# Front of a two-layer decoder trunk on one Trainium2 core: memory norms from rows, low parts on VectorE, keys in side banks, an earlier x

## The chip, the cores and the metric

The kernel runs on one core of a Trainium2 chip. The core has TensorE (PE, matrix multiply, with weight loads listed as PEld), VectorE (DVE), ScalarE (ACT), GpSimd (POOL) and SyncE (SP, which here issues loads), an on-chip memory SBUF of 128 partitions, and eight accumulator banks (PSUM) of 128 x 512 floats that PE writes and VectorE and ScalarE read. Each engine works through its own queue in order and waits on semaphores for the others. The metric is the device time of one execution in microseconds, as a median of several.

## What is computed

Two layers of a hybrid decoder trunk over a sequence of 256 tokens of width 1024, with 256 memory tokens. Per layer:

```python
h = rms_norm(x, norm_g[l])
proj = h @ w_in[l]                                  # 1024 x 5120: ten groups of 512 columns
q_a, k_a, v_a, q_h, f_h, i_h, q_m, z = jnp.split(proj, split_points, axis=-1)
...                                                 # o_a: causal attention; o_h: gated linear recurrence
kv_m = rms_norm(mem, mem_norm_g[l]) @ w_mem_kv[l]   # 1024 x 1024
k_m, v_m = jnp.split(kv_m, 2, axis=-1)
km = rms_norm(k_m.reshape(B, M, MEM_HEADS, MEM_HEAD_DIM), mem_k_norm[l])
vm = v_m.reshape(B, M, MEM_HEADS, MEM_HEAD_DIM)
...                                                 # o_m: attention of qm over km, vm
y = jnp.concatenate([o_a, o_h, o_m], axis=-1) * jax.nn.silu(z)
x = x + y @ w_out[l]
```

`rms_norm` divides each row by the root of its mean square. For the memory this factor (`rm` in the kernel) is one number per memory token. The kernel multiplies un-normalised memory with the weights and applies `rm` afterwards, to the values directly and to the keys inside their own norm.

## The kernel before

**Precision and tiles.** All products are made in three passes from a high part (rounded to the type `fp32r`) and a low part (the difference, rounded likewise). Every weight tile is 128 x 1024 floats (512 KB) and passes through three steps in a fixed order of tiles: a load by SyncE into one of four `wr` buffers (`dma_to`, L124), a cast on ScalarE into one of three `wh` buffers (`h_to`, L141, instructions at L147 and L150), and the low part on VectorE into one of three `wl` buffers (`l_to`, L153, instructions at L159 and L162). `slot` (L190) asks for loads five tiles, casts three tiles and low parts two tiles ahead of the tile in use. A load into a `wr` buffer waits until the low part of the tile four before is made.

**Order of the work.** The first eight tiles are the memory's key and value weights of layer 0 (`group_kv`): the memory, transposed on the host (`mem_t`) and split into `mTh` and `mTl` (`m_split`, L351 and L352), is the stationary operand; key columns go to two accumulator banks, value columns to two more. There are four main banks (`acc`) and four side banks (`sd`). In layer 0 keys and values both take main banks, so all four are taken; in layer 1 the keys take side banks. Then `group_a` makes the projection's forget gate and query of the recurrence, each in four column tiles of 128 columns, one main bank each; `g_sum` empties a bank. Eight more groups, the output projection, and the second layer follow.

**Side work.** Everything that is not a large product is a Python generator (`spawn`), advanced one step at each `slot`. It only sets the order in which the program is written; a planner then orders the instructions of each engine by its own estimate of their durations. Instructions marked with `keep_in_program_order` keep their order among themselves: all loads, the spread of the norm, and some others.

**The front's side work**, in the order that matters here:

- `g_norm0` (L399 to L435) makes `h` of layer 0. Squares of `x`'s rows with sums on ScalarE (L403), a scale on VectorE (`msx`, L411), a power on GpSimd (`rx`, L412), a diagonal on VectorE (`dg`, L417), one product with a matrix of ones on PE that spreads the row factors along the columns of a side bank (L420). Then for each of eight 128-column blocks VectorE multiplies the transposed `x` (`xc`, loaded from `x_t`) by gain and factor (L427), ScalarE makes the high part (L431) and GpSimd the low part (L432) of `hT`, the operand of every projection.
- `g_mem_r` (L371 to L397) makes `rm`. Squares of the transposed memory on ScalarE (L376), sums over blocks on GpSimd (L379, L381), four one-column products with ones on PE that sum over partitions, a scale on VectorE (L389), a power on GpSimd (L391). `rm2` (L393, L394) goes to the keys' norm.
- `g_km` (from L602) copies the keys out of their banks (L605 on VectorE, L606 on ScalarE), takes their norm, and transposes them on PE (L636). `g_vm` (from L644) waits for `rm` and empties the value banks (L650 on ScalarE, L651 on VectorE).

**Loads.** SyncE issues in program order: the memory and the first weight tiles interleaved, up to six weight tiles, then `x` in two halves, the first half of `x_t`, the seventh and eighth weight tile, the second half of `x_t`, and from there weight tiles as their buffers come free.

Of the kernel before, what the change touches and what calls it, by code (L numbers as in the profile page):

```python
# [12 lines left out]
F32 = mybir.dt.float32  # L13
# [9 lines left out]
D = 1024  # L23
# [19 lines left out]


@with_exitstack
def hymba_kernel(ctx: ExitStack, tc: tile.TileContext, x, x_t, mem_t, positions, w_in, w_out, w_mem_kv,
                 gains, moba_g, out):
    nc = tc.nc
    cst = ctx.enter_context(tc.tile_pool(name="cst", bufs=1))
# [13 lines left out]
    def room(what, n=1):  # L63
        while held[what] + n > room_of[what]:
            yield
# [9 lines left out]
    def side_tile():  # L75
        held["sd"] += 1
        assert held["sd"] <= 4
        return psum.tile([128, 512], F32, name="sd", tag="sd", bufs=4)

    def rel(what="sd", n=1):  # L80
        held[what] -= n
# [42 lines left out]
    def dma_to(n):  # L124
        while st["dma"] < min(n, len(chunks)):
            i = st["dma"]
            ap = chunks[i][1]
            raws[i] = sb.tile([128, 1024], F32, name="wr", tag="wr", bufs=RAW_BUFS)
            load(raws[i], ap)
            st["dma"] += 1  # L130
# [67 lines left out]
    def mm(o, a, b, s, e):  # L198
        nc.tensor.matmul(o, lhsT=a, rhs=b, start=s, stop=e)  # L199
# [89 lines left out]

    gT = cst.tile([128, NG], F32, name="gT")  # L290
    mraw = [sb.tile([128, 4, 256], F32, name=f"mraw{t}", tag=f"hq{t}", bufs=1) for t in range(2)]
    xs = sb.tile([128, 2, D], F32, name="xs")
    pos_i = cst.tile([128, 2], I32, name="pos_i")
    mg = cst.tile([128, 2, 2, 64], F32, name="mg")
# [10 lines left out]
    mem_load(2, 4)  # L305
    dma_to(3)
    mem_load(4, 8)
    dma_to(6)
    for t in range(2):
        load(xs[:, t], dram(x, t * 128 * D, [[D, 128], [1, D]]))  # L310
    xc = [sb.tile([128, 4, 256], F32, name="xc", tag=t, bufs=1) for t in ("PTh", "PTl")]
# [2 lines left out]
    for h in range(2):  # L314
        dma_to((6, 8)[h])
        load(xc[h], dram(x_t, h * 1024, [[2048, 128], [1, 1024]]))
    dma_to(8)

    def g_loads():
        while "hT0" not in done:  # L320
# [48 lines left out]
    hTh, hTl = hT[:, :, 0], hT[:, :, 1]  # L369

    def g_mem_r():  # L371
        while "mraw" not in done:
            yield
        yield 2
        for h in range(2):
            nc.scalar.activation(mraw[h], mraw[h], AF.Square)  # L376
            yield
        f0, f1 = (a.rearrange("p k s -> p (k s)") for a in mraw)
        nc.gpsimd.tensor_tensor(f0, f0, f1, op=OP.add)  # L379
        for n in (512, 256):  # L380
            nc.gpsimd.tensor_tensor(f0[:, :n], f0[:, :n], f0[:, n:2 * n], op=OP.add)  # L381
        yield 3
        yield from room("sd")
        ss = side_tile()
        for t in range(2):
            mm(ss[:, t:t + 1], f0[:, t * 128:(t + 1) * 128], T["ones"][:, 0:1], True, True)
        yield
        ms = small("msm", 2)
        nc.vector.tensor_scalar(ms, ss[:, :2], 1.0 / D, EPS, op0=OP.mult, op1=OP.add)  # L389
        rel()  # L390
        nc.gpsimd.tensor_tensor(rm, ms, pw[:, :2], op=OP.pow)  # L391
        yield 2
        nc.vector.reciprocal(rm2, ms)  # L393
        nc.vector.tensor_scalar(rm2, rm2, 1.0 / 128, None, op0=OP.mult)  # L394
        nc.vector.scalar_tensor_tensor(gkq, in0=gT[:, GR_MQ:GR_MQ + 2], scalar=128.0 ** -0.5,
                                       in1=gT[:, GR_MK:GR_MK + 2], op0=OP.mult, op1=OP.mult)
        done.add("rm")  # L397

    def g_norm0():  # L399
        sq = sb.tile([128, D], F32, name="sqx", tag="P", bufs=2)  # L400
        ss = small("ssx", 2)
        for t in range(2):
            nc.scalar.activation(sq, xs[:, t], AF.Square, accum_out=ss[:, t:t + 1])  # L403
        held["P"] += 1
        ones = sb.tile([128, 128], F32, name="ones", tag="sq", bufs=2)
        nc.gpsimd.memset(ones, 1.0)
        T["ones"] = ones
        yield 2
        ms = small("msx", 2)
        r = small("rx", 2)  # L410
        nc.vector.tensor_scalar(ms, ss, 1.0 / D, EPS, op0=OP.mult, op1=OP.add)  # L411
        nc.gpsimd.tensor_tensor(r, ms, pw[:, :2], op=OP.pow)  # L412
        rel("P")
        yield
        dg = sb.tile([128, 2, 128], F32, name="dg", tag="sg", bufs=2)
        for t in range(2):
            nc.vector.tensor_scalar(dg[:, t], ident, r[:, t:t + 1], None, op0=OP.mult)  # L417
        yield from room("sd")
        rb = side_tile()
        tc.keep_in_program_order(nc.tensor.matmul(rb[:, :256], lhsT=ones, rhs=dg.rearrange("p t s -> p (t s)"),  # L420
                                                  start=True, stop=True))
        yield
        for kp in range(5):
            if kp < 4:
                for k in (2 * kp, 2 * kp + 1):
                    xk, c = xc[k // 4][:, k % 4], GR_NORM + k
                    nc.vector.scalar_tensor_tensor(xk, in0=xk, scalar=gT[:, c:c + 1], in1=rb[:, :256],  # L427
                                                   op0=OP.mult, op1=OP.mult)
            if kp:
                ks, xp = slice(2 * kp - 2, 2 * kp), xc[kp // 3][:, (2 * kp - 2) % 4:(2 * kp - 2) % 4 + 2]  # L430
                nc.scalar.copy(hTh[:, ks], xp)  # L431
                nc.gpsimd.tensor_tensor(hTl[:, ks], xp, hTh[:, ks].bitcast(F32), op=OP.subtract)  # L432
            yield
        rel()
        rel("PTh")  # L435
        rel("PTl")
        done.add("hT0")
# [164 lines left out]
    def g_km(l, acc):  # L602
# [1 line left out]
        kn = sb.tile([128, 2, 512], F32, name="kn", tag="qk", bufs=1)  # L604
        nc.vector.tensor_copy(kn[:, 0], acc[0])  # L605
        nc.scalar.copy(kn[:, 1], acc[1])  # L606
        if l:
            rel("sd", 2)
        yield
        for t in range(2):  # L610
# [33 lines left out]
    def g_vm(l, acc):  # L644
        vmh = sb.tile([128, 2, 512], F32R, name="vmh", tag="vmh", bufs=1)
        vml = sb.tile([128, 2, 512], F32R, name="vml", tag="vml", bufs=1)
        while "rm" not in done:
            yield
        for t in range(2):
            nc.scalar.activation(vmh[:, t], acc[t], AF.Copy, scale=rm[:, t:t + 1])  # L650
            nc.vector.scalar_tensor_tensor(vml[:, t], in0=acc[t], scalar=rm[:, t:t + 1], in1=vmh[:, t].bitcast(F32),  # L651
                                           op0=OP.mult, op1=OP.subtract)
        T["vm"] = vmh, vml
        yield
# [566 lines left out]
    spawn(g_loads(), 5)  # L1221
    spawn(setup, 8)
    for l in range(DEPTH):
        group_kv(mTh, mTl, lambda a: g_km(l, a), lambda a: g_vm(l, a), side_tile if l else acc_tile)
        need(f"hT{l}")
        group_a(hT, lambda h, a: g_f(l, h, a))
        group_a(hT, lambda h, a: g_q(l, h, a))
        for gen in (g_ih, lambda l, a: g_qk(l, 1, a), lambda l, a: g_qk(l, 0, a), g_zh, A_, M_, g_qm, g_va):
            if gen in (A_, M_):
                group_a(hT, lambda h, a, br=gen: g_zt(l, br, h, a))  # L1230
            else:
                acc = group_b(hTh, hTl)
                spawn(gen(l, acc))
                slot(True)
        if l == 0:
            spawn(g_lb())
        w_out_phase(l)
        if l + 1 < DEPTH:
            spawn(g_norm(l + 1))
            slot(True)  # L1240
# [44 lines left out]
```

## Time and profile before

| what | us |
|---|---|
| median of three runs (lowest, highest) | 407.47 (407.43, 407.75) |
| profiled execution, whole | 407.73 |
| profiled execution, span of the trace | 405.9 |
| PE busy in the span | 398.6 |
| VectorE busy | 322.1 |
| ScalarE busy | 264.1 |
| GpSimd busy | 70.4 |

Times within the trace count from the start of the span. A line of the timeline reads: start, length, engine, line of the kernel, operation, tile written <- tiles read, shapes, count; in brackets the idle time of the engine before it and what ended it. Lengths of matmuls are modelled and overlap. A line of a group reads: count, total busy us, mean ns of one, and the idle time before. Times of GpSimd are rough.

### The profile page before, as it was taken

The numbers are of one execution on the slowest core, as the hardware profiler recorded it, in microseconds if no ns is written. First come the engines' busy times: TensorE is split into PE (matmuls) and PEld (weight loads), VectorE is DVE, ScalarE is ACT, GpSimd is POOL, SyncE is SP. The second block draws the span as 40 slices with busy tenths as digits, with TensorE's granted clock in tenths as the row PEclk, the third lists the DMA queues.
The fourth block names the chain that finished last, engine by engine and source line by source line (L and its number), as shares of the span: only waits on it lengthen the run. The fifth ranks groups of instructions, "written<-read, shape, count | busy, mean of one in ns | idle before, by whom it ended". The sixth has DMA issues, their size and how long they took to land.

```text
span 405.9 us, 7373 instructions
## 1 busy us (share of the span) xinstructions
PE 398.6 (98%) x2786; PEld 334.8 (82%) x2786; DVE 322.1 (79%) x618; ACT 264.1 (65%) x433; POOL 70.4 (17%) x87
## 2 busy tenths in 40 slices
PE   7999999999999999999999999999999999999996
PEld 5877888878899888888888888788788988888885
DVE  4899698789999786886576889679899997578654
ACT  5966676436976999664365866435487599976440
POOL 2466603165001002000000120004510100200000
PEclk9999999999999999999999999999999999999999
DMA  7966566546644445344446464554675442565302
GB/s 248 412 238 205 158 203 208 173 153 214 197 156 154 144 156 158 118 152 155 157 156 208 155 205 168 198 167 146 188 228 167 147 155 94 168 199 162 107 2 103
DMA packets 21796, 69.85 MB, mean 172 GB/s; under 512 B 2560, under 2 KB 4992, under 8 KB 21760
## 3 DMA queue, kind: packets, MB, share of 16 engines
q1 hardware_dynamic: 19296, 67.12, 49.9%
q10 hardware_dynamic: 2464, 2.25, 2.3%
q8 instruction: 22, 0.36, 0.4%
q14 instruction: 14, 0.11, 0.1%
HBM read 66.22 MB, written 1.05 MB: 166 GB/s over the span
## 4 chain that ended last, share of the span: by engine, by line
PE 87%; POOL 4%; DVE 4%; DMA 2%; issue 2%; ACT 1%; SPq 1%; POOLq 0%; DVEq 0%
PE acc L199 54%; PE acc L1169 16%; PE sd L199 9%; PE sd L203 2%; DMA wr<-in_w_mem_kv_dram 2%; PE sd L1044 1%; PE sd L1023 1%; PE sd L940 1%; POOL mraw L381 1%; PE sd L1132 1%; DVE xc L427 1%; POOL mk L579 1%; DVE wl L159 1%; POOL mraw L379 1%; ACT wh L150 1%
## 5 line engine op out<-in xcount | busy, mean ns | idle before, releaser
L147 ACT CAST wh<-wr 128x1024 fp32r<-128x1024 f32 x104 | 109.0, 1051 | 72.7 <-PE acc L199 45.3
L159 DVE TENSOR_TENSOR wl<-wr,wh 128x1024 fp32r<-128x1024 f32 x104 | 127.4, 1229 | 31.5 <-ACT wh L147 31.1
L199 PE MATMUL acc<-wh,hT 128*128 128x512 f32 x384 | 120.9, 393 | 0.0
L199 PE MATMUL acc<-hT,wh 128*128 128x512 f32 x256 | 91.0, 395 | 0.4 <-ACT kn L606 0.4
L199 PEld LDWEIGHTS acc<-wh,hT 128*128 128x128 f32 x384 | 71.5, 188 | 14.4
L199 PE MATMUL acc<-wl,hT 128*128 128x512 f32 x192 | 76.0, 396 | 0.0
L199 PE MATMUL acc<-hT,wl 128*128 128x256 f32 x256 | 72.6, 284 | 0.5 <-DVE wl L159 0.4
L199 PEld LDWEIGHTS acc<-hT,wh 128*128 128x128 f32 x256 | 48.0, 188 | 10.7 <-POOL hT L432 0.8
L199 PEld LDWEIGHTS acc<-hT,wl 128*128 128x128 f32 x256 | 48.4, 189 | 1.4 <-DVE wl L159 1.3
L199 PEld LDWEIGHTS acc<-wl,hT 128*128 128x128 f32 x192 | 36.1, 188 | 7.4
L162 DVE SCALAR_TENSOR_TENSOR wl<-wr,gT,wh 128x1024 fp32r<-128x1024 f32 (+1 forms) x17 | 23.9, 1419 | 9.0 <-ACT wh L150 6.8
L150 ACT ACTIVATE wh<-wr,gT 128x1024 fp32r<-128x1024 f32 (+1 forms) x17 | 18.4, 1098 | 10.8 <-PE acc L1169 3.1
L1169 PE MATMUL acc<-wl,yh 128*128 128x512 f32 x64 | 25.2, 394 | 0.0
L1169 PE MATMUL acc<-wh,yh 128*128 128x512 f32 x64 | 25.1, 402 | 0.0
L1169 PE MATMUL acc<-wh,yl 128*128 128x512 f32 x64 | 24.6, 394 | 0.0
L903 POOL TENSOR_TENSOR rka<-msa,pw 128x8 f32<-128x8 f32 x4 | 14.1, 3527 | 54.8 <-DVE msa L902 54.8
L199 PE MATMUL acc<-wh,mTh 128*128 128x512 f32 x48 | 18.9, 394 | 1.2 <-ACT wh L150 1.2
L1169 PE MATMUL acc<-wh,y 128*128 128x512 f32 (+1 forms) x64 | 20.0, 385 | 0.0
L199 PE MATMUL acc<-wh,mTl 128*128 128x512 f32 x48 | 18.7, 390 | 0.0
L1004 ACT ACTIVATE P<-P,nba,rq 128x128 f32<-128x128 f32 (+1 forms) x32 | 17.3, 542 | 0.1
L199 PE MATMUL acc<-wl,mTh 128*128 128x512 f32 x48 | 14.6, 392 | 0.0
L1169 PEld LDWEIGHTS acc<-wh,yl 128*128 128x128 f32 x64 | 12.0, 188 | 2.4
(238 smaller groups left out, 673.3 us busy)
## 6 DMA issues: line engine op xcount, KB each, us to landing
wr<-in_w_in_dram SPq DMA_DIRECT2D x80, 512.0 KB, 3.4
wr<-in_w_out_dram SPq DMA_DIRECT2D x24, 512.0 KB, 3.8
wr<-in_w_mem_kv_dram SPq DMA_DIRECT2D x15, 512.0 KB, 3.6
k<-k ACTq DMA_DIRECT2D x8, 256.0 KB, 3.7
xs<-in_x_dram SPq DMA_DIRECT2D x2, 512.0 KB, 6.7
xc<-in_x_t_dram SPq DMA_DIRECT2D x2, 512.0 KB, 7.4
out_dram<-xs SPq DMA_DIRECT2D x3, 256.0 KB, 2.0
mraw<-in_mem_t_dram SPq DMA_DIRECT2D x2, 256.0 KB, 5.4
```

The lines of the kernel that those rows point to most:

```text
L147: nc.scalar.copy(whs[i], raws[i])
L150: nc.scalar.activation(whs[i][:, sl], raws[i][:, sl], AF.Copy, scale=gT[:, g:g + 1])
L159: nc.vector.tensor_tensor(wls[i], raws[i], whs[i].bitcast(F32), op=OP.subtract)
L162: nc.vector.scalar_tensor_tensor(wls[i][:, sl], in0=raws[i][:, sl], scalar=gT[:, g:g + 1], in1=whs[i][:, sl].bitcast(F32), op0=OP.mult, op ...
L199: nc.tensor.matmul(o, lhsT=a, rhs=b, start=s, stop=e)
L203: tc.keep_in_program_order(nc.tensor.matmul(o, lhsT=a, rhs=b, start=True, stop=True))
L379: nc.gpsimd.tensor_tensor(f0, f0, f1, op=OP.add)
L381: nc.gpsimd.tensor_tensor(f0[:, :n], f0[:, :n], f0[:, n:2 * n], op=OP.add)
L427: nc.vector.scalar_tensor_tensor(xk, in0=xk, scalar=gT[:, c:c + 1], in1=rb[:, :256], op0=OP.mult, op1=OP.mult)
L903: nc.gpsimd.tensor_tensor(r[:, t8], ms[:, t8], pw[:, :8], op=OP.pow)
L1004: pin(nc.scalar.activation(P[:, i, kc[t]], P[:, i, kc[t]], AF.Exp, bias=nb[:, c:c + 1], scale=rq[:, r:r + 1], accum_out=sm[:, c:c + 1]))
L1169: ins = nc.tensor.matmul(a, lhsT=y, rhs=wt[:, cs], start=n == (0 if to is None else nk - 2) and j == 0, stop=n == nk - 1 and j == 2)
```

## The change

Five edits in the front of the kernel, of which one also holds for later uses of the same code:

1. The memory is also passed in its own row layout (`mem`). Two loads of 128 x 1024 floats, `memr`, are issued behind the eleventh weight tile, into the two buffers with the tag `P`. `g_mem_r` now waits until `hT0` is written in program order, and takes the row sums of squares on ScalarE with `accum_out`; the squares of the transposed memory, the three sums on GpSimd and the four products with ones on PE go. Scale, power and what follows stay.
2. The square of `x` in `g_norm0` writes to the buffer of the forget gate (`hF`) in place of one of the `P` buffers.
3. The low parts of `hT` in layer 0 are made by VectorE in place of GpSimd.
4. The keys of layer 0 go to side banks as those of layer 1 do, and `g_km` releases them in both.
5. The two loads of `x` are issued behind five weight tiles in place of six.

```diff
@@ -289,6 +289,8 @@
     mraw = [sb.tile([128, 4, 256], F32, name=f"mraw{t}", tag=f"hq{t}", bufs=1) for t in range(2)]
+    memr = [sb.tile([128, D], F32, name="memr", tag="P", bufs=2) for t in range(2)]
+    held["P"] += 2
@@ -305,7 +307,7 @@
     mem_load(4, 8)
-    dma_to(6)
+    dma_to(5)
     for t in range(2):
         load(xs[:, t], dram(x, t * 128 * D, [[D, 128], [1, D]]))
@@ -314,7 +316,9 @@
     for h in range(2):
         dma_to((6, 8)[h])
         load(xc[h], dram(x_t, h * 1024, [[2048, 128], [1, 1024]]))
-    dma_to(8)
+    dma_to(11)
+    for t in range(2):
+        load(memr[t], dram(mem, t * 128 * D, [[D, 128], [1, D]]))
@@ -369,25 +373,14 @@
     def g_mem_r():
-        while "mraw" not in done:
-            yield
-        yield 2
-        for h in range(2):
-            nc.scalar.activation(mraw[h], mraw[h], AF.Square)
-            yield
-        f0, f1 = (a.rearrange("p k s -> p (k s)") for a in mraw)
-        nc.gpsimd.tensor_tensor(f0, f0, f1, op=OP.add)
-        for n in (512, 256):
-            nc.gpsimd.tensor_tensor(f0[:, :n], f0[:, :n], f0[:, n:2 * n], op=OP.add)
-        yield 3
-        yield from room("sd")
-        ss = side_tile()
-        for t in range(2):
-            mm(ss[:, t:t + 1], f0[:, t * 128:(t + 1) * 128], T["ones"][:, 0:1], True, True)
-        yield
+        while "hT0" not in done:
+            yield
+        ss = small("ssm", 2)
+        for t in range(2):
+            tc.keep_in_program_order(nc.scalar.activation(memr[t], memr[t], AF.Square, accum_out=ss[:, t:t + 1]))
+        rel("P", 2)
         ms = small("msm", 2)
-        nc.vector.tensor_scalar(ms, ss[:, :2], 1.0 / D, EPS, op0=OP.mult, op1=OP.add)
-        rel()
+        nc.vector.tensor_scalar(ms, ss, 1.0 / D, EPS, op0=OP.mult, op1=OP.add)
         nc.gpsimd.tensor_tensor(rm, ms, pw[:, :2], op=OP.pow)
@@ -397,20 +390,17 @@
     def g_norm0():
-        sq = sb.tile([128, D], F32, name="sqx", tag="P", bufs=2)
+        sq = sb.tile([128, D], F32, name="sqx", tag="hF", bufs=1)
...
-        held["P"] += 1
...
-        rel("P")
@@ -429,7 +419,7 @@
                 nc.scalar.copy(hTh[:, ks], xp)
-                nc.gpsimd.tensor_tensor(hTl[:, ks], xp, hTh[:, ks].bitcast(F32), op=OP.subtract)
+                nc.vector.tensor_tensor(hTl[:, ks], xp, hTh[:, ks].bitcast(F32), op=OP.subtract)
@@ -604,7 +594,7 @@
-        if l:
+        if True:
             rel("sd", 2)
@@ -1221,7 +1211,7 @@
-        group_kv(mTh, mTl, lambda a: g_km(l, a), lambda a: g_vm(l, a), side_tile if l else acc_tile)
+        group_kv(mTh, mTl, lambda a: g_km(l, a), lambda a: g_vm(l, a), side_tile)
@@ -1264,7 +1254,7 @@
-        "x": v["x"], "x_t": columns(v["x"]), "mem_t": columns(v["mem"]),
+        "x": v["x"], "x_t": columns(v["x"]), "mem": v["mem"], "mem_t": columns(v["mem"]),
```

More of the change, by code (lines that the diff above doesn't have):

```diff
@@ L45, in hymba_kernel @@
 @with_exitstack
-def hymba_kernel(ctx: ExitStack, tc: tile.TileContext, x, x_t, mem_t, positions, w_in, w_out, w_mem_kv,
+def hymba_kernel(ctx: ExitStack, tc: tile.TileContext, x, x_t, mem, mem_t, positions, w_in, w_out, w_mem_kv,
                  gains, moba_g, out):
@@ L403, in g_norm0 @@
             nc.scalar.activation(sq, xs[:, t], AF.Square, accum_out=ss[:, t:t + 1])
-        held["P"] += 1
         ones = sb.tile([128, 128], F32, name="ones", tag="sq", bufs=2)
         nc.gpsimd.memset(ones, 1.0)
-        T["ones"] = ones
         yield 2
```

## The prediction, made before the result was known

> **What bounds the kernel now.** I read the page first, then the stretches, then TensorE's timeline, and last the engines that release it.
>
> ```profile
> span 405.9 us, 7373 instructions
> ...
> PE 87%; POOL 4%; DVE 4%; DMA 2%; issue 2%; ACT 1%; SPq 1%; POOLq 0%; DVEq 0%
> ```
>
> The second line is the chain of work that ended last: nearly all TensorE (PE). By stretches of the span (busy time per engine, then clock, DMA share, GB/s):
>
> ```profile
> 25.00:30.00 5.00, 5.00 (x24) 3.99 (x22) 5.00 (x11) 3.70 (x6) 3.76 (x3) 1.00 0.39 116
> 30.00:35.00 5.00, 4.13 (x22) 3.06 (x21) 5.00 (x7) 4.23 (x8) 5.00 (x4) 1.00 0.72 241
> 100.00:200.00 100.00, 100.00 (x614) 85.90 (x614) 80.19 (x168) 74.81 (x139) 4.04 (x3) 1.00 0.48 155
> ```
>
> In the body PE is busy throughout; this change can win nothing there. At 30 to 35 us PE is idle for 0.87 us, while VectorE (third busy time) and GpSimd (fifth) are full. So the end moves by what PE gains in the front and by nothing else. How fast PE can go, from its timeline around the third column tile of the first projection:
>
> ```profile
> 36.83 0.39 PE L199 MATMUL acc<-hT,wh 128*128 128x512 f32 x1
> 37.06 0.28 PE L199 MATMUL acc<-hT,wl 128*128 128x256 f32 x1
> 37.17 0.39 PE L199 MATMUL acc<-hT,wh 128*128 128x512 f32 x1
> 37.62 0.39 PE L199 MATMUL acc<-hT,wl 128*128 128x256 f32 x1
> ```
>
> Printed lengths overlap, so I count from start to start: 0.23 us behind a 512-wide matmul, 0.11 behind a 256-wide one. The last pair is 0.45 apart: 0.22 lost. The same count at the other places, first at the norm of x, then where the first projection begins:
>
> ```profile
> 22.72 0.61 PE L199 MATMUL acc<-wl,mTh 128*128 128x512 f32 x2
> 23.67 0.67 PE L420 MATMUL sd<-dg,ones 128*128 128x256 f32 x2 [0.33 <-DVE dg L417]
> 24.18 0.50 PE L199 MATMUL sd<-ones,mraw 128*128 128x1 f32 x4
> 24.54 0.48 PE L199 MATMUL acc<-wh,mTh 128*128 128x512 f32 x1
> ```
> ```profile
> 29.64 0.61 PE L199 MATMUL acc<-wl,mTh 128*128 128x512 f32 x2
> 30.69 0.47 PE L199 MATMUL acc<-hT,wh 128*128 128x512 f32 x1 [0.44 <-ACT kn L606]
> 31.60 0.39 PE L199 MATMUL acc<-hT,wl 128*128 128x256 f32 x1 [0.43 <-DVE wl L159]
> ```
>
> The memory matmuls end their issue at 22.72 + 0.46 = 23.18; the matmul that spreads the norm of x starts at 23.67: 0.49 lost on `dg`. The four one-column sums of the memory norm hold PE from 24.18 to 24.54: 0.36. At 29.64 + 0.46 = 30.10 PE could start the projection and starts at 30.69: 0.59, waiting for ScalarE to empty a key bank. Behind that first matmul it waits for the low part of the ninth weight tile: 31.60 - 30.69 - 0.23 = 0.68. The wait list for 20 to 50 us has one more:
>
> ```profile
> PE sd L636 <- DVE kn L625: 0.5, 2, 0.3
> ```
>
> That is the transposes of the memory keys near 48 us.
>
> **The change part by part.** (1) *Memory norms from rows.* It removes two ScalarE squares of 128x1024, three GpSimd adds, and the four PE sums: **0.36** of PE by the rows above. The adds, with what follows on GpSimd:
>
> ```profile
> 15.71 2.55 POOL L379 TENSOR_TENSOR mraw<-mraw,mraw 128x1024 f32<-128x1024 f32 x1 [12.24 <-ACT mraw L376]
> 18.34 3.84 POOL L381 TENSOR_TENSOR mraw<-mraw 128x512 f32<-128x512 f32 x2
> 22.28 0.73 POOL L412 TENSOR_TENSOR rx<-msx,pw 128x2 f32<-128x2 f32 x1
> ```
>
> The power for the norm of x starts as the adds end, so they sit in the path to `dg`. They also slow VectorE, as the five low parts of 128x1024 from 14 us on show (min/median/max ns):
>
> ```profile
> L162 DVE SCALAR_TENSOR_TENSOR wl<-wr,gT,wh x5: 1280/2257/2645, 14.7 to 26.4; 128x1024 fp32r<-128x1024 f32 x5
> ```
>
> Undisturbed 1.28, beside GpSimd up to 2.65: the three longer ones lose at least 0.98, 0.98 and 1.37. Two of them lie under the adds and give back some 2.3 us of VectorE. [...]
>
> (2) *x behind five weight tiles.* The front's transfers are back to back, as the answer for 14 to 24 us says:
>
> ```profile
> DMA packets 1115, 4.07 MB, mean 407 GB/s; under 512 B 121, under 2 KB 121, under 8 KB 1115
> ```
>
> A tile of 512 KB takes 524,288 / 407 = 1.29 us, and landings follow the order of issue. x passes one tile, so it lands 1.29 earlier, and the sixth weight tile 2.58 later. Its ScalarE work:
>
> ```profile
> L403 ACT ACTIVATE sqx<-xs x2: 1041/1052/1062, 17.6 to 18.8; 128x1024 f32<-128x1024 f32 x2
> L403 ACT ACTIVATION_READ_ACCUMULATOR sqx<-xs x2: 184/184/184, 18.6 to 19.7; 128x1 f32 x2
> ```
>
> The squares can move up by about 1.3, since the memory squares are gone too, and the power waits for no add. The chain to `dg` has to gain 0.49 and gains more than twice that: **0.49** saved. The late weight tile takes x's old place, which had landed when the second square began at 18.8; its cast has a row of its own (count, busy, mean ns):
>
> ```profile
> L150 ACT ACTIVATE wh<-wr,gT 128x1024 fp32r<-128x1024 f32 x7 | 7.9, 1147 | 2.3 <-DMA wr<-in_w_mem_kv_dram 2.2
> ```
>
> So it is cast by 18.8 + 1.15 = 20.0. PE starts that tile's twelve matmuls 12 x 0.23 ahead of 23.18, at 20.4. This costs nothing while 0.4 us of cover lasts, and one for one beyond.
>
> (3) *Low parts of h by VectorE.* GpSimd's four, and the same shape on VectorE (the memory's low parts):
>
> ```profile
> L432 POOL TENSOR_TENSOR hT<-xc,hT x4: 1294/1786/2275, 26.2 to 32.7; 128x512 fp32r<-128x512 f32 x4
> ```
> ```profile
> L352 DVE TENSOR_TENSOR mTl<-mraw,mTh 128x512 fp32r<-128x512 f32 x4 | 2.7, 688 | 0.2 <-ACT mTh L351 0.2
> ```
>
> VectorE takes on 4 x 0.69 = 2.75 us. What it loses by, and gets back, in its full stretch:
>
> ```profile
> 26.37 2.26 DVE L162 SCALAR_TENSOR_TENSOR wl<-wr,gT,wh 128x1024 fp32r<-128x1024 f32 x1
> 28.55 1.64 DVE L427 SCALAR_TENSOR_TENSOR xc<-xc,gT,sd 128x256 f32<-128x256 f32 x4
> 30.12 0.15 DVE L393 RECIPROCAL rm<-msm 128x2 f32<-128x2 f32 x1
> 30.19 1.35 DVE L159 TENSOR_TENSOR wl<-wr,wh 128x1024 fp32r<-128x1024 f32 x1
> 31.47 0.68 DVE L605 COPY kn<-acc 128x512 f32<-128x512 f32 x1
> 32.07 1.71 DVE L159 TENSOR_TENSOR wl<-wr,wh 128x1024 fp32r<-128x1024 f32 x1
> 33.70 1.26 DVE L394 TENSOR_SCALAR rm<-rm 128x2 f32<-128x2 f32 x1
> ```
>
> Against 1.28 for a 1024-wide low part and 0.15 for a tiny one: 0.98 + 0.07 + 0.43 + 1.11 = 2.6 us back. VectorE's work in this stretch stays level, and with (2) it begins the products of x earlier. So the ninth tile's low part should be there when PE asks: I take **0.68** and the **0.22** at 37.4 as saved. Bounds: none of the 0.90, or all and the 0.5 at the key transposes too (their chain runs over VectorE and GpSimd); I leave the transposes as they are.
>
> (4) *Keys in side banks.* The first projection tile no longer waits for the key copies: **0.59**. Two of four side banks are held until the copies, the spread of the norm takes a third; the transposes that want side banks come behind the copies.
>
> (5) *Rows loaded late.* Two loads of 512 KB go behind the eleventh weight tile, which before was issued and landed (last row: us to landing):
>
> ```profile
> 24.75 0.33 SPq L122 DMA_DIRECT2D wr<-in_w_in_dram  x1
> ```
> ```profile
> DMA to landing us min/median/max: 4.2/4.2/4.2
> ```
>
> At the latest by this row the rows land at 24.75 + 4.2 + 2 x 1.29 = 31.5; if the seventh tile's low part frees its buffer earlier, about 30. In SyncE's queue their two issues stand in front of the twelfth tile's, which waits for a buffer and is wanted only by the fourth projection tile: no cost. On ScalarE's in-order queue the two squares stand in front of casts for the projection. The rows' own buffers are idle until the attention, and so is the one that the square of x moves into until the forget gates: nothing waits for either. Then the tail to the two accumulator banks that hold the memory values:
>
> ```profile
> L650 ACT ACTIVATE vmh<-acc,rm x2: 692/697/702, 30.4 to 31.5; 128x512 fp32r<-128x512 f32 x2
> L651 DVE SCALAR_TENSOR_TENSOR vml<-acc,rm,vmh x2: 740/740/741, 34.9 to 35.7; 128x512 fp32r<-128x512 f32 x2
> L391 POOL TENSOR_TENSOR rm<-msm,pw x1: 1690/1690/1690, 27.5 to 27.5; 128x2 f32<-128x2 f32 x1
> ```
>
> From landing: square and sum 1.24, scalar 0.15, power 0.73 to 1.69, `vmh` 0.70, `vml` 0.74: 3.6 to 4.5 us, so a value bank is free between 33.6 and 36.0. The third projection tile would want it at 37.17 - 0.49 - 0.36 - 0.59 - 0.68 = 35.05, unless it takes the bank of the first tile. The wait is worth 0 to 1 us; I charge 0.3, nearer the end at which the other banks help.
>
> *Sum:* 0.36 + 0.49 + 0.59 + 0.68 + 0.22 - 0.3 = 2.04, about 2. The profiled execution took 407.73 (span 405.9, 1.8 around it), 0.26 above the median 407.47 of three runs. 407.73 - 2.04 = 405.7; from the median **405.4**.
>
> **The rivals.** *B, more goes:* the transposes' 0.5 vanish too and the bank wait is nothing: 2.04 + 0.5 + 0.3 = 2.84, 404.6, and a little lower if the planner also packs the front tighter. For it: GpSimd is relieved. Against: the key chain still has its own GpSimd work.
>
> *C, VectorE becomes the bound:* its 2.75 us of new work does not fit, the 0.90 stays and between a fifth and a half of the new work, 0.55 to 1.4, falls on PE: 0.36 + 0.49 + 0.59 = 1.44 less that is 0.89 to 0.04: 406.6 to 407.4. For it: VectorE is full from 25 to 35 us and now carries the whole path from the norm to h. Against: the 2.6 us returned.
>
> *D, the rows come too late (slower):* ScalarE stands at the squares with the projection's casts behind it, and the value banks stay held. It decides against the change when a bank comes free later than 35.05 + 2.34 = 37.4 (2.34 being the sum without the charge), that is with rows landing after about 33. At 34.5 the banks are free at 39.0: 2.34 saved, 3.95 lost, 409.1. For it: the rows are last in SyncE's queue, behind a load that waits for a buffer. Against: from 25 to 30 us the transfers take 0.39 of the DMA engines, so little stands in the rows' way once issued.
>
> *E, nothing moves:* instruction order comes from a planner with its own idea of durations; it can put the spread of the norm earlier on PE and wait as long there. The sums' 0.36 remain: 407.1 to 407.6.
>
> **How the numbers follow.** Forecast 0.50 (405.4, between 404.8 and 406.2), B 0.17, C 0.16, D 0.09, E 0.08. About 0.2% (0.8 us) is what a measurement of this kernel can tell from no change. Faster by more: forecast, B, and a third of C: 0.72. Within: the rest of C and nearly all of E: 0.19. Slower: D: 0.09. Leaving out D, E and the upper half of C above, and B's extreme below, the range is 404.0 to 407.0.
>
> **What would show it.** Right: no one-column matmuls; low parts near 1.28 throughout 14 to 35 us; the spread of the norm without a wait; the projection's first matmul directly behind the memory's last, near 29.2; PE above 4.8 of 5 at 30 to 35. Wrong: PE waiting for `hT` or `wl` by VectorE (C), for `vmh`/`vml` or a cast behind the squares (D), for `dg` (E), or new waits in the body.

## The result, and the profile after

| | before | after |
|---|---|---|
| median of seven runs, us | 407.65 | 404.9 |
| lowest to highest, us | 407.43 to 407.75 | 404.46 to 406.65 |
| profiled execution, us | 407.73 | 404.87 |
| its span, us | 405.9 | 403.1 |

The ratio of the times is 0.9937, with a 95% interval of 0.9927 to 0.9948: 2.75 us faster, where about 2 had been forecast (405.4, range 404.0 to 407.0). The direction and the range held. That the pieces of the sum did not all come from where the sum had them is the subject of what follows.

The page of the changed kernel: span, busy time with its share and the number of instructions by engine, and the chain of work that ended last. Lines of its code lie some ten below those of the kernel before.

```profile
span 403.1 us, 7356 instructions
...
PE 397.2 (99%) x2782; PEld 334.4 (83%) x2782; DVE 318.8 (79%) x622; ACT 265.1 (66%) x435; POOL 54.6 (14%) x80
...
PE 96%; DVE 2%; DMA 1%; ACT 0%; issue 0%; SPq 0%; DVEq 0%; ACTq 0%
```

GpSimd, which had 4% of the chain, is no longer in it, and PE went from 87% to 96%. The two stretches of the front (columns: the span of the stretch, PE, PEld, DVE, ACT, POOL busy, clock, DMA share, GB/s):

```profile
25.00:30.00 5.00, 5.00 (x25) 4.18 (x24) 5.00 (x9) 4.12 (x6) 0.00 (x0) 1.00 0.93 342
30.00:35.00 5.00, 4.93 (x29) 3.96 (x28) 5.00 (x12) 4.94 (x10) 0.89 (x5) 1.00 0.78 287
```

At 30 to 35 us PE is busy for 4.93 in place of 4.13. From 25 to 30 us GpSimd does nothing, and the DMA engines, at 0.39 before, are at 0.93: the rows land here, and the stretch that the prediction read as free is nearly full. The wait list of PE for 6 to 60 us has one line left, at the very start, between the warm-up products and the first product of the memory; the kernel before has it too (1.2):

```profile
PE sd L199 <- ACT wh L150: 1.3, 1, 1.3
```

PE's timeline of the changed kernel at the places that the prediction counted (start, length, engine, line, operation):

```profile
19.86 0.61 PE L199 MATMUL acc<-wl,mTh 128*128 128x512 f32 x2
20.32 0.59 PE L410 MATMUL sd<-dg,ones 128*128 128x256 f32 x2
...
28.05 0.39 PE L199 MATMUL acc<-hT,wh 128*128 128x512 f32 x1
...
29.18 0.39 PE L199 MATMUL acc<-hT,wh 128*128 128x512 f32 x1
...
34.53 0.28 PE L199 MATMUL acc<-hT,wl 128*128 128x256 f32 x1
34.88 0.50 PE L199 MATMUL acc<-hT,wh 128*128 128x512 f32 x1
...
46.16 0.60 PE L626 MATMUL sd<-ident,kn 128*128 128x128 f32 x4
...
52.74 0.39 PE L199 MATMUL acc<-wh,hT 128*128 128x512 f32 x1
...
399.30 0.28 PE L1159 MATMUL sd<-wh,y 128*128 128x256 f32 x1
```

The spread of the norm (`dg`) starts 0.46 behind a pair of 512-wide matmuls, that is at once. There are no one-column sums. The projection's first matmul slips in among the last memory matmuls at 28.05; its next ones follow from 29.18 on. One new loss stands at the third projection tile: 34.88 - 34.53 - 0.11 = 0.24. The transposes of the keys (L626) run at 46.16 without a stop. In the kernel before they looked like this, with the two ends of the comparison below them:

```profile
47.22 0.39 PE L199 MATMUL acc<-hT,wh 128*128 128x512 f32 x1
47.94 0.66 PE L636 MATMUL sd<-ident,kn 128*128 128x128 f32 x4 [0.33 <-DVE kn L625]
48.75 0.66 PE L636 MATMUL sd<-ident,kn 128*128 128x128 f32 x4 [0.15 <-DVE kn L625]
49.16 0.37 PE L199 MATMUL acc<-hT,wl 128*128 128x256 f32 x1
...
55.96 0.39 PE L199 MATMUL acc<-wh,hT 128*128 128x512 f32 x1
...
402.34 0.28 PE L1169 MATMUL sd<-wh,y 128*128 128x256 f32 x1
```

The transposes lost 47.94 - 47.22 - 0.23 = 0.49, and between the two fours, where four in a row take 49.16 - 48.75 = 0.41, another 48.75 - 47.94 - 0.41 = 0.40: 0.89, not the 0.5 of the wait list. The list counts only the time in which an engine shows idle; the printed lengths of matmuls run on into the wait.

**The account.** Gone: 0.36 (sums) + 0.49 (`dg`) + 0.59 (key bank) + 0.68 + 0.22 (ninth weight tile) + 0.89 (transposes) = 3.23. New: 0.24. That leaves 2.99. The third group's first product (`acc<-wh,hT`) comes at 52.74 in place of 55.96: 3.22 earlier; the other 0.2 lies in steps of 0.1 to 0.2. At the last matmul 402.34 - 399.30 = 3.04 are left, and at the end of the span 405.9 - 403.1 = 2.8. So some 0.2 is given back over 350 us of body and some 0.2 behind the last matmul.

### The profile page after: what moved, and what is told of

It is laid out like the page before. It is cut to its first block, busy times and chain, and to the rows that moved or that the text cites. A ratio compares the mean times of both kernels' runs of the same rounds, so it can differ in the third digit from the quotient of the medians.

```text
span 403.1 us, 7356 instructions
## 1 busy us (share of the span) xinstructions
PE 397.2 (99%) x2782; PEld 334.4 (83%) x2782; DVE 318.8 (79%) x622; ACT 265.1 (66%) x435; POOL 54.6 (14%) x80
## 4 chain that ended last, share of the span: by engine, by line
PE 96%; DVE 2%; DMA 1%; ACT 0%; issue 0%; SPq 0%; DVEq 0%; ACTq 0%
PE acc L199 59%; PE acc L1159 16%; PE sd L199 11%; PE sd L203 2%; PE sd L1034 1%; PE sd L1013 1%; DMA wr<-in_w_mem_kv_dram 1%; PE sd L930 1%; PE sd L1122 1%; DVE wl L159 1%; PE sd L450 0%; PE sd L1068 0%; PE sd L750 0%; PE sd L626 0%; DVE ssk L583 0%; DVE hT L422 0%
## 5 line engine op out<-in xcount | busy, mean ns | idle before, releaser
L162 DVE SCALAR_TENSOR_TENSOR wl<-wr,gT,wh 128x1024 fp32r<-128x1024 f32 (+1 forms) x17 | 20.6, 1219 | 7.4 <-ACT wh L150 4.9
L1159 PE MATMUL acc<-wh,yl 128*128 128x512 f32 x64 | 24.8, 397 | 0.0
L199 PE MATMUL sd<-wh,mTh 128*128 128x512 f32 x32 | 12.9, 405 | 1.3 <-ACT wh L150 1.3
L1159 PEld LDWEIGHTS acc<-wl,yh 128*128 128x128 f32 x64 | 12.0, 188 | 2.4
L1159 PEld LDWEIGHTS acc<-wh,yh 128*128 128x128 f32 x64 | 11.9, 188 | 2.5 <-issue 0.3
```

The source lines that it names most:

```text
L162: nc.vector.scalar_tensor_tensor(wls[i][:, sl], in0=raws[i][:, sl], scalar=gT[:, g:g + 1], in1=whs[i][:, sl].bitcast(F32), op0=OP.mult, op ...
L1159: ins = nc.tensor.matmul(a, lhsT=y, rhs=wt[:, cs], start=n == (0 if to is None else nk - 2) and j == 0, stop=n == nk - 1 and j == 2)
```

## The experiments

Twelve kernels ran, on three chips. Ratios are to the kernel before as measured on the same chip (408.08, 407.49 and 407.55 us). "PE's loss" is counted from start to start in the profiled execution, between 20 and 60 us.

| run | kernel | median us | ratio (95%) | PE's losses of 0.3 or more |
|---|---|---|---|---|
| u1 | changed, old memory norm | 406.67 | 0.9967 (0.9954 to 0.9979) | 1.02 low part |
| u3 | changed, low parts of `hT` on GpSimd | 405.41 | 0.9934 (0.9922 to 0.9946) | 0.99 `hT` |
| u4 | changed, keys in main banks | 405.01 | 0.9929 (0.9915 to 0.9944) | 0.38 key bank |
| u5 | changed, x behind six | 409.19 | 1.0028 (1.0016 to 1.004) | 2.17 bank, 1.11 + 0.47 low parts, then a clock of 0.53 |
| u15 | changed, old memory norm and x behind six | 406.81 | 0.9985 (0.9976 to 0.9993) | 0.86 + 0.45 low parts |
| a1 | before, memory norm from rows | 411.04 | 1.0086 (1.0073 to 1.0099) | 3.26 bank, 0.78 key bank, 0.46 low part, then a clock of 0.50 |
| a3 | before, low parts of `hT` on VectorE | 406.77 | 0.9982 (0.9973 to 0.999) | 0.95 low part, 0.52 `dg`, 0.38 key bank |
| a5 | before, x behind five | 406.84 | 0.9986 (0.9978 to 0.9995) | 0.48 + 0.87 key banks, 0.30 low part |
| v_x_six | u5, values copied out at once | 406.44 | 0.9979 (0.9971 to 0.9987) | 1.11 + 0.84 low parts |
| v_changed | changed, values copied out at once | 404.42 | 0.9933 (0.992 to 0.9946) | none of 0.2 |
| r13 | changed, rows behind thirteen tiles | 407.18 | 0.9992 (0.9982 to 1.0001) | 1.13 + 1.30 + 0.62 banks |
| w26 | changed, longer warm-up | 404.66 | 0.9933 (0.9921 to 0.9944) | none of 0.2 |

The trace of a5 begins with a slow start of PE (last section): by 10.3 us seven matmuls, some 1.6 us, are missing. In u15's PE is busy for 400.0 us, against 398.3 in u1 with as many matmuls. What these two rows list are the waits of a PE that comes late, and a wait that is missing in them may be missing for that reason.

### One part undone at a time

The theory was the prediction's: each edit carries its own term, so undoing it gives that term back.

**u1: the old memory norm.**

```diff
-    dma_to(11)
-    for t in range(2):
-        load(memr[t], dram(mem, t * 128 * D, [[D, 128], [1, D]]))
+    dma_to(8)
...
+            nc.scalar.activation(mraw[h], mraw[h], AF.Square)
...
+        nc.gpsimd.tensor_tensor(f0, f0, f1, op=OP.add)
...
+            mm(ss[:, t:t + 1], f0[:, t * 128:(t + 1) * 128], T["ones"][:, 0:1], True, True)
```

> The changed kernel with the memory norm as before (squares of the transposed memory, three GpSimd sums, four one-column products; no row loads). Theory (each edit releases a wait of its own, and the waits add up): TensorE gets the four products back (0.36), waits for the norm of x again (up to 0.49), and the fourth and fifth weight tiles' low parts run beside the sums at 2.3 to 2.6 us instead of 1.28: 405.5 to 406.2, that is 0.6 to 1.3 above the changed kernel's 404.9. Rival (one cause, GpSimd's reads beside VectorE, makes nearly all of the gain): 406.8 or more. Rival (the sums were hidden): at most 0.36 above.

PE's wait list from 6 to 60 us without the line of the start, and the group of the memory's low parts on VectorE from 13 to 30 us (duration min/median/max in ns):

```profile
PE acc L199 <- DVE wl L159: 0.9, 1, 0.9
```
```profile
L162 DVE SCALAR_TENSOR_TENSOR wl<-wr,gT,wh x5: 1272/1279/2644, 14.3 to 26.0; 128x1024 fp32r<-128x1024 f32 x5
```

Against the changed kernel it costs (0.9967 - 0.9937) x 408.08 = 1.2 us. That size held. Its make-up did not: no wait for `dg` came back, since x is early in this kernel; the loss is the sums' 0.36 and a low part 1.02 late, on a VectorE that with the adds back has a low part of 2644 ns again (the changed kernel's longest: 1285).

**u3: low parts of `hT` back on GpSimd.**

```diff
-                nc.vector.tensor_tensor(hTl[:, ks], xp, hTh[:, ks].bitcast(F32), op=OP.subtract)
+                nc.gpsimd.tensor_tensor(hTl[:, ks], xp, hTh[:, ks].bitcast(F32), op=OP.subtract)
```

> The changed kernel with the low parts of h made by GpSimd again. Theory: low parts of weight tiles in 20 to 35 us run beside GpSimd at 1.7 to 2.3 us again, the ninth tile's comes late and TensorE waits 0.5 to 1.4 us at the start of the projection: 405.4 to 406.3. Rival (VectorE is so much ahead once x is early that it does not matter which engine makes them): 404.7 to 405.2. Rival (VectorE as the bound, so that GpSimd's help is worth something): below 404.6.

```profile
PE acc L199 <- POOL hT L422: 0.8, 1, 0.8
```

The line, from PE's wait list, is a wait that the changed kernel doesn't have, and the profiled span is 403.7 against 403.1. The ratio, 0.9934, is not above the changed kernel's. On the same chip u4 took 405.01 against 405.41 here. A loss between 0 and 0.6 us fits all of this; of the 0.5 to 1.4 expected all but the low end is excluded, and more isn't settled.

**u4: layer 0's keys back in main banks.**

```diff
-        if True:
+        if l:
             rel("sd", 2)
...
-        group_kv(mTh, mTl, lambda a: g_km(l, a), lambda a: g_vm(l, a), side_tile)
+        group_kv(mTh, mTl, lambda a: g_km(l, a), lambda a: g_vm(l, a), side_tile if l else acc_tile)
```

> The changed kernel with layer 0's keys in main banks. Theory: the first projection matmul waits for a key copy again, 0.6 us: 405.3 to 405.7, and the value banks, which are freed near 39 us, now stand with nothing beside them but the key banks, so a later tile may wait as well: up to 406.5. Rival (the planner fills the wait with other memory products): 404.9 to 405.1.

```profile
PE acc L199 <- ACT kn L596: 0.2, 1, 0.2
```

The wait for a key bank comes back, 0.38 from start to start, and the wait at the third tile is gone in exchange. Nothing is lost in the span (403.1) or in the ratio.

**u5: x behind six weight tiles.**

```diff
-    dma_to(5)
+    dma_to(6)
     for t in range(2):
         load(xs[:, t], dram(x, t * 128 * D, [[D, 128], [1, D]]))
```

> The changed kernel with x behind six weight tiles. Theory: x lands 1.28 later, the norm's factor reaches the products of x 1.3 later, and VectorE, busy from 21 to 37 us, is 1.3 later with the low parts of h; about half of it shows on TensorE: 405.2 to 405.9. Rival (the cover was there: x's chain had slack): 404.8 to 405.1.

This fell badly: 409.19, slower than the kernel before, when 405.2 to 405.9 had been expected. PE's timeline, then ScalarE's and VectorE's, of this run:

```profile
36.27 0.28 PE L199 MATMUL acc<-hT,wl 128*128 128x256 f32 x1
38.56 0.63 PE L199 MATMUL acc<-hT,wh 128*128 128x512 f32 x1 [2.01 <-DVE as L284]
```
```profile
35.78 1.05 ACT L147 CAST wh<-wr 128x1024 fp32r<-128x1024 f32 x1 [1.86 <-PE acc L199]
36.73 0.36 ACT L283 COPY al<-acc 128x256 f32<-128x256 f32 x1
...
38.21 1.28 ACT L640 ACTIVATE vmh<-acc,rm 128x512 fp32r<-128x512 f32 x2
```
```profile
36.87 1.23 DVE L159 TENSOR_TENSOR wl<-wr,wh 128x1024 fp32r<-128x1024 f32 x1
...
38.10 0.41 DVE L284 TENSOR_TENSOR as<-acc,al 128x256 f32<-128x256 f32 x1
```

The third projection tile starts at 38.56, when `as` (38.10 + 0.41) has emptied the bank of the first tile. `as` stands behind a low part on VectorE and needs `al`. `al` stands on ScalarE behind a cast that waits 1.86 us for PE to release a `wh` buffer. The other candidates, the two value banks, wait for `rm`, and `vmh` only starts at 38.21. So all four main banks are held, two by the values and two by projection tiles, and the one that would come free first has its copy behind a cast.

A new theory, **the bank theory**, came of this: the late rows hold the value banks until past 37 us; what saves the changed kernel is that the copy `al` comes early in ScalarE's queue, and it does so only with x early. Against it stood the additive reading (u5 lost its x term and something unrelated).

### The bank theory tried

**a1: only the memory norm from rows, on the kernel before** (edits 1 and 2).

> The kernel before with the memory norm from rows alone (x behind six tiles, keys in main banks, low parts by GpSimd). Theory (banks): the sums' 0.36, the wait for the norm of x (0.5) and GpSimd's disturbance go, but the value banks are held to about 40 us and a projection tile waits some 2 us: 1.002 to 1.006 of the kernel before. Rival (the edits add up): 0.9 us gained, 0.998.

```profile
39.08 0.80 PE L199 MATMUL acc<-hT,wh 128*128 128x512 f32 x1 [3.09 <-DVE as L284]
```
```profile
35.21 1.05 ACT L147 CAST wh<-wr 128x1024 fp32r<-128x1024 f32 x1 [1.21 <-PE acc L199]
36.17 0.63 ACT L283 COPY al<-acc 128x256 f32<-128x256 f32 x2
```

Timelines of PE and of ScalarE: the same picture, with the copy behind a cast that waits for PE. The part by itself makes the kernel 0.86% slower, more than the bank theory's own figure, because the wait is 3.26 in place of some 2 and because the granted clock is 0.50 behind it (last section). The additive reading, which would have this part gain, fell.

**u15: old memory norm and x behind six**, so that only edits 3 and 4 are left.

> The changed kernel with both the old memory norm and x behind six tiles, so that only the low parts on VectorE and the keys in side banks are left of the change. Theory (banks): the 2.2 us wait of the run with x behind six tiles comes from the value banks, which the late rows hold until about 41 us; with the old norm they come free near 36, the wait goes, and what is left are about 1 us of waits for VectorE: 0.995 to 1.000 of the kernel before. Rival (x's place alone decides, by a late VectorE): 1.003 or more, as with the rows.

No wait for a bank in PE's list; 406.81, ratio 0.9985. x behind six costs nothing like 4 us where the values' banks are freed early. The first value bank is free at 35.5, more than 1.7 us before the third tile, so a PE on time would have found it too. Held.

**a5: only x behind five, on the kernel before.**

> The kernel before with x behind five tiles alone. Theory: GpSimd's sums still end at 22.2 and the power for the norm of x stands behind them, so x's earlier landing is not used: 0.998 to 1.001 of the kernel before. Rival (x's place is worth the 4 us by itself that its undoing cost): 0.990 to 0.994.

0.9986, in the band expected, but not for its reason: x's earlier landing is used. What x's earlier place gains, the key banks partly take: the first two projection tiles wait 0.48 and 0.87 for them, where the kernel before loses 0.59. The wait for `dg` is gone even with GpSimd's sums in place, for the power for x now gets in ahead of the last of them, as GpSimd's timeline shows (PE is late in this trace; in u1's, where it isn't, the wait is gone too):

```profile
20.63 0.72 POOL L412 TENSOR_TENSOR rx<-msx,pw 128x2 f32<-128x2 f32 x1
21.33 0.74 POOL L381 TENSOR_TENSOR mraw<-mraw 128x256 f32<-128x256 f32 x1
```

**v_x_six: u5 with the value banks emptied at once.** ScalarE and VectorE each copy one bank of values to a spare buffer as soon as PE is done; scaling by `rm` comes later, from the copy.

```diff
+        vr = sb.tile([128, 2, 512], F32, name="vr", tag="ih", bufs=1)
+        nc.scalar.copy(vr[:, 0], acc[0])
+        nc.vector.tensor_copy(vr[:, 1], acc[1])
+        yield
         while "rm" not in done:
             yield
...
-            nc.scalar.activation(vmh[:, t], acc[t], AF.Copy, scale=rm[:, t:t + 1])
+            nc.scalar.activation(vmh[:, t], vr[:, t], AF.Copy, scale=rm[:, t:t + 1])
```

> The changed kernel with x behind six tiles, and the values of both layers copied out of their banks at once (one copy on ScalarE, one on VectorE, about 0.6 us each) and scaled from the copy later. Theory (banks): the 2.2 us wait for a bank goes; the other waits of that run (1.1 and 0.5 for weight tiles' low parts) stay or grow by the copy: 0.996 to 0.999 of the kernel before, against 1.0028. Rival (the bank was only where a late VectorE showed): 1.001 or more.

The decisive run. ScalarE's timeline, then PE's whole list of waits for a low part:

```profile
36.20 1.06 ACT L147 CAST wh<-wr 128x1024 fp32r<-128x1024 f32 x1 [1.99 <-PE acc L199]
37.16 0.36 ACT L283 COPY al<-acc 128x256 f32<-128x256 f32 x1
```
```profile
PE acc L199 <- DVE wl L159: 1.6, 2, 0.9
```

The cast waits for PE as before and the copy is even later, at 37.16. But PE doesn't wait for it: the third tile takes a value bank, which is free. The ratio goes from 1.0028 to 0.9979, some 2.0 us (u5's figure contains the low clock behind the wait, 0.53 in its profiled execution), with the late low parts of u5 still there, the second of them grown from 0.47 to 0.84. The bank theory held in its first part; that the early copy is what saves the changed kernel stays a reading of the traces.

**r13: the changed kernel with its rows two weight tiles later** (`dma_to(13)` in place of `dma_to(11)`), x left early. This is rival D's own mechanism, tried by itself.

> The changed kernel with the rows loaded behind thirteen weight tiles in place of eleven. Theory (a bank is emptied by in-order queues): the rows land 3 to 5 us later, near 34 to 36; ScalarE stands at their squares with the copies behind them that empty the first projection tiles' banks, the value banks are no help, and a tile waits 1 to 3 us: 0.996 to 1.002 of the kernel before, more if the wait passes 2 us and TensorE's clock drops. Rival (with x early the first tiles' banks are emptied in time whatever the rows do): 0.9925 to 0.9945, as the changed kernel.

```profile
36.27 1.06 ACT L380 ACTIVATE memr<-memr 128x1024 f32<-128x1024 f32 x1 [2.89 <-DMA memr<-in_mem_dram]
```
```profile
PE acc L199 <- DVE as L284: 2.1, 2, 1.1
...
PE acc L199 <- DVE vml L641: 0.5, 1, 0.5
```

ScalarE stands 2.89 us at the first square, with casts and copies behind it, and PE waits for a bank three times. The second wait is the one that the theory names: `al` comes at 38.26, behind a cast behind the square. The first, at 35.77, is not: there `al` was early, at 33.01, and `as` stood behind a low part on VectorE until 35.30. 407.18, ratio 0.9992: most of the gain is lost (2.2 of 2.6 us by the ratios), and the granted clock stayed up (0.998 or more in all twelve executions).

### The rest

**a3: only the low parts of `hT` on VectorE, on the kernel before.**

> The kernel before with the low parts of h on VectorE alone. Theory (VectorE and GpSimd exclude each other): VectorE takes 2.75 us and gets about 2.6 back, TensorE's waits at the start of the projection stay within 0.5 us of what they were: 0.9985 to 1.0015. Rival (VectorE the bound): 1.002 to 1.004. Rival (a gain by itself): 0.998 or less.

0.9982, slightly better than expected, but not for the reason of the prediction. The waits it was credited with grow: for the ninth tile's low part 0.95 in place of 0.68, for another low part 0.26 in place of 0.22. With `dg` at 0.52 and the key bank at 0.38 the four come to 2.11, where the kernel before loses 1.98. What it gains is the transposes' 0.89: 0.89 - 0.13 = 0.76, and 407.55 - 406.77 = 0.78 was measured. VectorE is busy for 322.6 us in place of 322.1: of the 2.75 that it took on, some 2.2 came back, where the theory had 2.6.

**v_changed: the changed kernel with the value banks emptied at once**, as in v_x_six.

> The changed kernel with the values copied out of their banks at once and scaled from the copy later. Theory: the one bank wait that is left (0.23) goes and the two copies hide: 0.992 to 0.994 of the kernel before (the changed kernel 0.9937). Rival: VectorE, which is full from 25 to 35 us, is late with a low part because of the copy: 0.995 or more.

The last bank wait is gone; PE has no loss of 0.2 or more left from the first product to 60 us. The median, 404.42, is the lowest of all, but 0.9933 (0.992 to 0.9946) can't be told from the changed kernel's 0.9937.

**w26: more warm-up products ahead of the first real one** (`WARM = 26` in place of 22), against single long executions that the last section tells of.

> The changed kernel with 26 warm-up products in place of 22, so that TensorE is idle for about 0.5 us before the first memory product and not for 1.2. Theory (the few executions about 1.7 us above the rest are those in which TensorE runs at half speed for its first 3.6 us of memory products): they become rarer, the median stays at 0.992 to 0.995 of the kernel before. Rival: as many of them as before (3 in about 25 over the kernels with an undisturbed middle), or the median rises because the warm-up ends behind the first weight tile.

404.57 to 404.82 in five executions, none long; with one long one in seven of the changed kernel, five are too few to say that it helps. The edit also did less than expected: PE's idle time ahead of the first product went from 1.28 to 1.00 us, not to 0.5.

## Why the prediction was right, and where it wasn't

- **"The end moves by what PE gains in the front and by nothing else": right.** 3.2 us gained by 53 us, 2.8 at the end. What is lost on the way (0.2 in the body, 0.2 behind the last matmul) was not in the forecast. The terms that the prediction did add up came to 0.36 + 0.49 + 0.59 + 0.68 + 0.22 - 0.24 = 2.10 in the trace, near its 2.04; what it fell short by is the transposes.
- **Sums, 0.36: right.** No such products are left.
- **`dg`, 0.49: right, and either edit is enough for it:** x's place with the sums back (u1), and the sums gone with x late (a1, u5). The squares of x moved further than the 1.3 worked out: ScalarE starts them at 15.03 and 16.37 in place of 17.6 and 18.8.
- **Ninth tile's low part, 0.68 + 0.22: gone, wrongly credited.** The prediction gave it to VectorE's new work fitting in. The low parts on VectorE don't remove it (a3: 0.95) and with GpSimd it doesn't come back (u3's new wait is for `hT`). With x early and the adds still there it is 1.02 (u1), with the adds gone and x late 1.11 (u5). It takes both. In the changed kernel all low parts take what an undisturbed one does:

```profile
L162 DVE SCALAR_TENSOR_TENSOR wl<-wr,gT,wh x5: 1275/1278/1285, 13.7 to 26.6; 128x1024 fp32r<-128x1024 f32 x5
```

  It had been 1280/2257/2645, and u1, with the adds back, has one of 2644. In the kernel before, five low parts of 128x1024 start on VectorE while an add or a low part runs on GpSimd, and each ends 1.1 us behind GpSimd's: at 19.35, 21.59, 28.63, 31.54 and 33.78, where GpSimd's end at 18.26, 20.50, 27.55, 30.46 and 32.69. One such pair:

```profile
26.24 1.31 POOL L432 TENSOR_TENSOR hT<-xc,hT 128x512 fp32r<-128x512 f32 x1 [3.10 <-ACT hT L431]
...
26.37 2.26 DVE L162 SCALAR_TENSOR_TENSOR wl<-wr,gT,wh 128x1024 fp32r<-128x1024 f32 x1
```

  That reads as a wait for GpSimd; which instructions of the two engines do so beyond these, no run shows. Nor does a run show the 2.6 us that VectorE was to get back, on which 0.68 and 0.22 rested: by its busy time in a3 it got some 2.2, and PE waited for the low part all the same.
- **Key bank, 0.59: gone, but worth nothing by itself in the changed kernel** (u4). The wait that the side banks spare at 29 us is 0.38 there, and the wait at the third tile, 0.24, takes its place.
- **The rows' charge, 0.3: right in size (0.24), wrong in its bank.** The prediction had a value bank free between 33.6 and 36.0. The group of the changed kernel that empties them (first and last start behind the durations):

```profile
L640 ACT ACTIVATE vmh<-acc,rm x2: 680/684/689, 36.9 to 37.5; 128x512 fp32r<-128x512 f32 x2
L641 DVE SCALAR_TENSOR_TENSOR vml<-acc,rm,vmh x2: 733/734/736, 38.1 to 38.8; 128x512 fp32r<-128x512 f32 x2
```

  They come free at 38.8 and 39.5, behind the 37.4 from which rival D was to decide. Yet D didn't decide, because the third tile took the bank of the first, the way out that the prediction named in half a sentence and didn't follow. ScalarE, then VectorE, in the changed kernel:

```profile
32.45 1.05 ACT L380 ACTIVATE memr<-memr 128x1024 f32<-128x1024 f32 x1
...
33.49 0.36 ACT L283 COPY al<-acc 128x256 f32<-128x256 f32 x1
33.74 1.05 ACT L147 CAST wh<-wr 128x1024 fp32r<-128x1024 f32 x1
```
```profile
32.99 1.27 DVE L583 TENSOR_REDUCE ssk<-sq 128x4 f32<-128x512 f32 x2
...
34.41 0.41 DVE L284 TENSOR_TENSOR as<-acc,al 128x256 f32<-128x256 f32 x1
```

  Here the copy stands ahead of the cast, where in u5 and a1 it stands behind one that waits for PE. That order was written by the planner; why it came out so was not tried. The late value banks also had a plain part: the rows, issued at 24.3 and 24.8, needed 5.3 us (median of the two), more than the 4.2 us of the tile that the prediction went by:

```profile
L122 SPq DMA_DIRECT2D memr<-in_mem_dram x2: 422/424/425, 24.3 to 24.8; - x2
...
DMA to landing us min/median/max: 4.9/5.3/5.7
```

  They landed by 30.5, inside the bound of 31.5. The tail, worked out as 3.6 to 4.5 us, took 8.3 to the first bank: the second square stands behind the squares of the keys, the power on GpSimd (36.16) behind small set-up operations, `vmh` waits for that power, and `vml` stands behind a low part.
- **Transposes, "I leave the transposes as they are": the step that failed.** They were the largest single piece, 0.89, priced at 0.5 from the wait list and left out. Their wait is in none of the twelve runs. Where it came from stands in the kernel before, in GpSimd's timeline and then VectorE's:

```profile
42.16 2.47 POOL L579 TENSOR_SCALAR mk<-xf 128x32 uint8<-128x32 f32 x5
44.71 1.67 POOL L620 TENSOR_TENSOR rk<-msk,pw 128x8 f32<-128x8 f32 x1
```
```profile
47.19 0.69 DVE L625 TENSOR_TENSOR kn<-kn,rk 128x512 f32<-128x512 f32 x1 [3.24 <-POOL rk L622]
```

  The power `rk` of the keys' norm has its input from VectorE at 40.4, but starts at 44.7, for in GpSimd's queue it stands behind small set-up operations, the masks `mk` last; VectorE, which scales the keys by it, idles 3.24 us, and the transposes come behind that. In a5, where GpSimd has the same work and only x moved, the power stands ahead of the masks (40.19), and the keys are scaled from 43.5 on. In the changed kernel the masks are still ahead, but end at 40.8, and the keys are scaled from 43.4 on. So the place in GpSimd's queue, more than GpSimd's load, fits all three; this is read from the traces, and no run changed that place by itself. Rival B had the waits vanish, for GpSimd's relief. Its 2.84 lies near the measured 2.75 partly by luck: it has the transposes 0.39 too low and the bank wait, 0.24, at nothing.
- **Rivals.** C (VectorE as the bound) and E (nothing moves) did not come. D didn't come, but is real: a1, u5 and r13 are D, on the kernel before, with x late, and with the rows late. Its price was not one for one either: where PE waited 2 to 3 us, the granted clock was 0.50 (a1) and 0.53 (u5) behind the wait in the profiled executions, and the mean clock of the run is 0.992 to 0.996 in all executions of a1 and 0.995 or 0.996 in half of u5's.
- **The additive sum.** The forecast is right as a total, but a1, a3 and a5 alone are worth +0.86%, -0.18% and -0.14%, together slower by half a per cent, while the whole is 0.63% faster (edit 4 was not run alone). Memory norms from rows are worth 1.2 us of gain in the changed kernel (u1) and 3.55 us of loss in the one before (a1, 411.04 - 407.49).

## What to carry to other kernels

Work out for each accumulator bank which instruction empties it and what stands ahead of that instruction in its engine's in-order queue; a copy behind a cast that itself waits for PE came, with the value banks held, with a bank wait of 2.17 us in u5 and of 3.26 in a1. A factor that arrives late need not hold accumulators: copy them out at once and scale the copy (some 2.0 us against u5; where the order of a queue happened to be good, as in the changed kernel, nothing that could be measured). Edits that share queues and banks are measured together and by leaving one out, and a wait on the matrix engine is counted from start to start.

## What the runs showed of the hardware

**A wait of 2 us in u5 cost more than 2 us.** u5's stretches before and after its wait (PE's matmuls in brackets, clock in the third column from the end):

```profile
33.00:36.00 3.00, 3.00 (x19) 2.62 (x18) 3.00 (x8) 1.14 (x3) 2.90 (x6) 1.00 0.79 223
...
38.60:42.20 3.60, 3.60 (x12) 3.01 (x12) 3.60 (x7) 3.32 (x5) 3.43 (x9) 0.53 0.78 271
```

At full clock 19 matmuls start in 3 us, so 23 would in 3.6; here 12 do, at a granted clock of 0.53. That is some 11 x 0.16 = 1.7 us on top of the wait. u5's twelve executions fall in two groups by the mean granted clock of the run: six at 0.995 or 0.996 took 409.8 to 410.3, six at 0.999 or 1.000 took 408.3 to 408.6, 1.5 us apart. All five of a1, whose wait is 3.1 us in the profiled one, have 0.992 to 0.996. The waits of up to 1.3 us in r13 brought no such drop (0.998 or more). Why only some executions of u5 have the drop, no run shows; how long PE waits in the others was not profiled. In the profiled one, with 2.01 us of idle, the clock was still 1.00 from 38.0 to 38.5, then 0.64 for 1 us, 0.50 for two and 0.65 for one, and 1.00 again from 42.5: in sum some 3.4 us at 0.50. In a1's trace it lasted longer: read in stretches of half a us, the clock was 0.94 from 37.5 and 0.50 from 38.0, some 2 us into the wait, and 0.73 from 44.5. That is some 6.8 us of half clock, 5.7 of them behind the wait.

**In a5 the start was slow without the clock column saying so.** The profiled execution of a5 was its longest (408.23, median 406.84). Its first stretch, and the same stretch of the changed kernel (PE's matmuls in the first brackets):

```profile
6.70:10.30 3.60, 3.60 (x9) 2.83 (x10) 2.59 (x4) 2.32 (x3) 0.00 (x0) 1.00 1.00 367
```
```profile
6.70:10.30 3.60, 3.60 (x16) 2.97 (x17) 2.58 (x4) 2.65 (x4) 0.00 (x0) 1.00 1.03 390
```

Nine matmuls in place of sixteen, at a clock given as 1.00: 7 x 0.23 = 1.6 us, about what that run is above its median. In the profiled execution of u15 (407.72, median 406.81) PE is busy for 1.7 us more than in u1's with as many matmuls (400.0 and 398.3), and the products `sd<-wh,mTh` take 418 ns in the mean, against 399. The one long execution of the changed kernel, 406.65, is 1.75 above its median; that it has the same cause is likely by its size, but it wasn't profiled.
